# Average pooling over 536 MB: rows of 128 KB per partition, and every store in SyncE's queue

## The chip, the core and the metric

The kernel runs on one core of a Trainium2 chip. A core has a VectorE (DVE in the profile), a ScalarE (ACT), a GpSimd (POOL), a TensorE (PE, not used here) and a SyncE (SP), and sixteen DMA engines which move data between the DRAM and the core's own memory of 128 partitions. SyncE and ScalarE each have a DMA queue; a transfer put into either is spread over all sixteen DMA engines. The metric is the time of one execution in microseconds (us); the time given is the median of several executions. A profile of one further execution shows where the time goes.

## The reference

Each row of 8192 numbers is cut into groups of four, and each group is replaced by its mean. The input is 64 x 256 x 8192 float32 (536.87 MB), the output 64 x 256 x 2048 float32 (134.22 MB).

```python
def reference(x, kernel_size, stride):          # kernel_size = stride = 4
    batch, channels, length = x.shape
    out_len = (length - kernel_size) // stride + 1
    output = np.zeros((batch, channels, out_len), dtype=np.float32)
    for i in range(out_len):
        start = i * stride
        output[:, :, i] = np.mean(x[:, :, start : start + kernel_size], axis=2)
    return output
```

Since windows do not overlap and 8192 is a multiple of 4, the whole input can be treated as one flat line of numbers: every four neighbours give one output.

## The kernel before

The flat input is cut into 64 blocks of 8 MB. In a block each of the 128 partitions holds a run of `RUN` = 16384 numbers, 64 KB, and the runs of neighbouring partitions follow each other in DRAM, so a block is one contiguous stretch (line 35). Its output is 16 KB for each partition, 2 MB in all (line 36).

For a block there are four steps. `load` (line 41) takes a tile `xt` of 64 KB per partition out of a pool of two (line 38) and has SyncE issue the transfer (line 44). `sums` (line 47) has VectorE add neighbours twice: first 16384 numbers to 8192, written over the first half of `xt` itself (line 50), then 8192 to 4096, written into a result tile `r` (line 54). `scale` (line 58) has ScalarE multiply by a quarter in place (line 59). Then the result is stored.

Result tiles hold two blocks, 32 KB per partition, and come from a pool of two (line 39). The loop (line 68) goes over pairs of blocks. In the first four pairs (`SINGLES` = 8 blocks) each block is scaled and stored by itself, 2 MB, from ScalarE's queue (lines 74 and 75). In the others the pair is scaled by one call and stored by one transfer of 4 MB from ScalarE's queue (lines 77 and 78); in that transfer each partition has two rows of 16 KB, which lie 2 MB apart in DRAM (`both`, line 65).

The last three transfers of results are arranged otherwise. The pair of blocks 60 and 61 is scaled and stored late, from SyncE's queue, behind the last loads (lines 86 and 87). Block 62 is stored by itself (line 90). Block 63 is loaded in two pieces of 40 KB and 24 KB per partition (`LAST`, lines 84 and 85), and each piece is summed, scaled and stored as soon as it can be (lines 91 to 95).

The order on each engine is that of the program; waits between engines are put in by the framework from what each instruction reads and writes. So a load into a tile of `xt` waits until VectorE has finished both sums of the block that was in it two loads before, a scale waits for VectorE, a store for ScalarE, and VectorE's second sum waits until the result tile has been stored from its use two pairs before.

Of the kernel before, what the change touches and what calls it, by code (L numbers as in the profile page):

```python
# [1 line left out]

# [4 lines left out]


RUN = 16384

SINGLES = 8
LAST = (10240, 6144)


@with_exitstack
def kernel(
    ctx: ExitStack,
    tc: tile.TileContext,
    x: bass.AP,
    kernel_size: bass.AP,  # L20
    stride: bass.AP,
    out: bass.AP,
):
    nc = tc.nc
    K, S = int(kernel_size), int(stride)
    assert K == S == 4
    B, C, L = x.shape
    P = nc.NUM_PARTITIONS
    dt = x.dtype
    M = RUN // K  # L30
    blocks = B * C * L // (P * RUN)
    assert blocks * P * RUN == B * C * L and L % K == 0 and blocks % 2 == 0
    assert sum(LAST) == RUN

    xb = x.rearrange("b c l -> (b c l)").rearrange("(n p m) -> n p m", p=P, m=RUN)
    ob = out.rearrange("b c l -> (b c l)").rearrange("(n p m) -> n p m", p=P, m=M)

    pin = ctx.enter_context(tc.tile_pool(name="xin", bufs=2))
    pout = ctx.enter_context(tc.tile_pool(name="res", bufs=2))

    def load(i, a=0, b=RUN, xt=None):
        if xt is None:
            xt = pin.tile([P, RUN], dt, name="xt")
        nc.sync.dma_start(out=xt[:, a:b], in_=xb[i][:, a:b])
        return xt

    def sums(o, xt, a=0, b=RUN):
        v = xt[:, a:b].rearrange("p (m k) -> p m k", k=2)
        h = xt[:, a : (a + b) // 2]
        nc.vector.tensor_tensor(  # L50
            out=h, in0=v[:, :, 0], in1=v[:, :, 1], op=mybir.AluOpType.add
        )
        w = h.rearrange("p (m k) -> p m k", k=2)
        nc.vector.tensor_tensor(  # L54
            out=o, in0=w[:, :, 0], in1=w[:, :, 1], op=mybir.AluOpType.add
        )

    def scale(o):
        nc.scalar.mul(o, o, 1.0 / K)  # L59

    def edges(cuts):
        at = [sum(cuts[:j]) for j in range(len(cuts) + 1)]
        return list(zip(at[:-1], at[1:]))

    def both(i):
        return ob[i : i + 2].rearrange("n p m -> p n m")

    for i in range(0, blocks - 2, 2):
        r = pout.tile([P, 2, M], dt, name="r")
        for h in range(2):  # L70
            xt = load(i + h)
            sums(r[:, h, :], xt)
            if i < SINGLES:
                scale(r[:, h, :])
                nc.scalar.dma_start(out=ob[i + h], in_=r[:, h, :])
        if SINGLES <= i < blocks - 4:
            scale(r[:])
            nc.scalar.dma_start(out=both(i), in_=r[:])

    n = blocks - 1  # L80
    t = pout.tile([P, 2, M], dt, name="r")
    xt = load(n - 1)
    xl = None
    for a, b in edges(LAST):
        xl = load(n, a, b, xl)
    scale(r[:])
    nc.sync.dma_start(out=both(n - 3), in_=r[:])
    sums(t[:, 0, :], xt)
    scale(t[:, 0, :])
    nc.sync.dma_start(out=ob[n - 1], in_=t[:, 0, :])  # L90
    for a, b in edges(LAST):
        o = t[:, 1, a // K : b // K]
        sums(o, xl, a, b)
        scale(o)
        nc.sync.dma_start(out=ob[n][:, a // K : b // K], in_=o)


# [1 line left out]
_INS = ['x', 'kernel_size', 'stride']  # L99
_OUTS = [((64, 256, 2048), 'float32')]  # L100

_NUMBERS = {'kernel_size': 4, 'stride': 4}


# [26 lines left out]
```

## Time and profile before

| | |
|---|---|
| median of three runs | 1554.46 us (1554.44 to 1555.88) |
| the profiled execution | 1554.4 us |
| its span, from first to last instruction | 1552.6 us |
| bytes moved by DMA, and their rate over the span | 671.12 MB, 432 GB/s |
| first sum, `xt` from 128 x 16384 to 128 x 8192 | 63 times, 8692 ns each |
| second sum, into `r`, 128 x 4096 | 63 times, 4425 ns each |
| scale of two blocks, 128 x 8192 | 27 times, 7029 ns each |
| scale of one block, 128 x 4096 | 9 times, 3616 ns each |
| load of a block, from issue to landing | median 35.1 us |
| store of 4 MB from ScalarE's queue, from issue to landing | median 52.0 us |
| idle time of VectorE that a load ended | 696.1 us, 63 times |

The span is the time between the first and the last instruction on the core; the profiled execution's own time is 1.8 us longer. Busy times of engines overlap each other, so they are not added up. Of a DMA the profile shows the issue (a short instruction on the issuing engine), the packets (one for each contiguous piece that a DMA engine moves) and the landing. A queue's share is the time of its packets as a part of sixteen engines' span. In the profile, "q1" is SyncE's queue and "q10" ScalarE's.

### The profile page before, as it was taken

To read this page: it belongs to the slowest core of one execution; us is meant where nothing else is said; L and a number is where in the kernel's file an instruction comes from. 1 tells how busy PE (TensorE), PEld (TensorE's weight loads), DVE (VectorE), ACT (ScalarE), POOL (GpSimd) and SP (SyncE) were. 2 spreads that over 40 slices of the span, in tenths; PEclk is the share of its full clock that TensorE was granted. 3 is DMA by queue.
4 is the path that set the end of the run, shared out by engine and by line. 5 is a ranking of instruction groups with operands and counts; after the bars stand their busy time and mean duration, and the time that the engine had idled before them with its cause. 6 is when DMAs were issued, how large, how long until landed. Compare 5 with 4: busy or idle time off the path is not lost.

```text
span 1552.6 us, 471 instructions
## 1 busy us (share of the span) xinstructions
DVE 839.7 (54%) x130; ACT 227.4 (15%) x39; POOL 0.2 (0%) x4
## 2 busy tenths in 40 slices
DVE  3646556546465464654646546455464554645646
ACT  1111101110111101111011110111101111011111
POOL 0000000000000000000000000000000000000000
DMA  9999999999999999999999999999999999999999
GB/s 417 420 434 438 439 439 439 412 445 444 413 433 435 443 438 439 432 424 429 439 438 433 437 434 419 439 432 438 439 419 434 434 437 439 441 423 442 422 440 400
DMA packets 18292, 671.12 MB, mean 432 GB/s; under 512 B 1649, under 2 KB 1649, under 8 KB 1777
## 3 DMA queue, kind: packets, MB, share of 16 engines
q1 hardware_dynamic: 10064, 545.26, 81.1%
q10 hardware_dynamic: 8224, 125.83, 18.9%
q14 instruction: 4, 0.02, 0.0%
HBM read 536.87 MB, written 134.22 MB: 432 GB/s over the span
## 4 chain that ended last, share of the span: by engine, by line
DMA 71%; DVE 28%; issue 0%; ACT 0%; DVEq 0%
DMA xt<-in_x_dram 71%; DVE xt L50 18%; DVE r L54 9%; ACT r L59 0%; DVEq L54 0%
## 5 line engine op out<-in xcount | busy, mean ns | idle before, releaser
L50 DVE TENSOR_TENSOR xt<-xt 128x8192 f32<-128x8192 f32 (+1 forms) x65 | 556.5, 8561 | 696.1 <-DMA xt<-in_x_dram 696.1
L59 ACT ACTIVATE r<-r 128x8192 f32<-128x8192 f32 (+3 forms) x38 | 226.2, 5951 | 1313.0 <-DVE r L54 1313.0
L54 DVE TENSOR_TENSOR r<-xt 128x4096 f32<-128x4096 f32 (+1 forms) x65 | 283.4, 4360 | 3.9
L59 ACT ACT_TABLE_LOAD x1 | 1.3, 1283 | 0.7 <-PEq L112 0.7
L112 POOL MEMSET const-bfloat16-1.0<- 128x1 bf16 x1 | 0.1, 101 | 0.0
L112 POOL MEMSET const-uint8-127<- 128x1 uint8 x1 | 0.1, 101 | 0.0
L112 POOL MEMSET const-float32-0.0<- 128x1 f32 x1 | 0.1, 98 | 0.2 <-issue 0.2
L112 POOL MEMSET const-float32-1.0<- 128x1 f32 x1 | 0.1, 98 | 0.0
## 6 DMA issues: line engine op xcount, KB each, us to landing
out_dram<-r ACTq DMA_DIRECT2D x26, 4096.0 KB, 52.0
out_dram<-r ACTq DMA_DIRECT2D x8, 2048.0 KB, 31.7
xt<-in_x_dram SPq DMA_DIRECT2D x1, 5120.0 KB, 23.1
out_dram<-r SPq DMA_DIRECT2D x1, 4096.0 KB, 33.0
xt<-in_x_dram SPq DMA_DIRECT2D x1, 3072.0 KB, 30.0
out_dram<-r SPq DMA_DIRECT2D x1, 2048.0 KB, 16.9
out_dram<-r SPq DMA_DIRECT2D x1, 1280.0 KB, 12.9
xt<-in_x_dram SPq DMA_DIRECT2D x63, 35.1
```

The lines of the kernel that those rows point to most:

```text
L50: nc.vector.tensor_tensor(out=h, in0=v[:, :, 0], in1=v[:, :, 1], op=mybir.AluOpType.add)
L54: nc.vector.tensor_tensor(out=o, in0=w[:, :, 0], in1=w[:, :, 1], op=mybir.AluOpType.add)
L59: nc.scalar.mul(o, o, 1.0 / K)
L112: nc = _bacc.Bacc("TRN2", target_bir_lowering=False, num_devices=1)
```

## The change

The input is cut into 32 groups of 16 MB. In a group each partition holds a run of 128 KB of neighbouring numbers, and two loads fetch it: the first takes the first 64 KB of every partition's run, the second the second 64 KB. So the rows of one load now start 128 KB apart in DRAM and are no longer one contiguous stretch. The group's output is 32 KB per partition in one piece, and the 4 MB of a group are contiguous.

Each half is scaled by a call of its own, the groups at the start too. All stores are issued by SyncE; ScalarE issues no transfer any more. A group's store is held back and issued after the second load of the next group. At the end, the last group's second half is again loaded in pieces of 40 KB and 24 KB; behind these loads come the store of group 30, that of the first half of group 31, and those of the two pieces. The two sums, the tiles of `xt` and the sizes of the pools are as before.

```diff
--- before.py
+++ after.py
@@ -8,7 +8,6 @@
 
 RUN = 16384
 
-SINGLES = 8
 LAST = (10240, 6144)
 
 
@@ -28,20 +27,24 @@
     P = nc.NUM_PARTITIONS
     dt = x.dtype
     M = RUN // K
-    blocks = B * C * L // (P * RUN)
-    assert blocks * P * RUN == B * C * L and L % K == 0 and blocks % 2 == 0
+    groups = B * C * L // (2 * P * RUN)
+    assert groups * 2 * P * RUN == B * C * L and L % K == 0
     assert sum(LAST) == RUN
 
-    xb = x.rearrange("b c l -> (b c l)").rearrange("(n p m) -> n p m", p=P, m=RUN)
-    ob = out.rearrange("b c l -> (b c l)").rearrange("(n p m) -> n p m", p=P, m=M)
+    xb = x.rearrange("b c l -> (b c l)").rearrange(
+        "(n p h m) -> n h p m", p=P, h=2, m=RUN
+    )
+    ob = out.rearrange("b c l -> (b c l)").rearrange(
+        "(n p m) -> n p m", p=P, m=2 * M
+    )
 
     pin = ctx.enter_context(tc.tile_pool(name="xin", bufs=2))
     pout = ctx.enter_context(tc.tile_pool(name="res", bufs=2))
 
-    def load(i, a=0, b=RUN, xt=None):
+    def load(g, h, a=0, b=RUN, xt=None):
         if xt is None:
             xt = pin.tile([P, RUN], dt, name="xt")
-        nc.sync.dma_start(out=xt[:, a:b], in_=xb[i][:, a:b])
+        nc.sync.dma_start(out=xt[:, a:b], in_=xb[g, h][:, a:b])
         return xt
 
     def sums(o, xt, a=0, b=RUN):
@@ -62,37 +65,34 @@
         at = [sum(cuts[:j]) for j in range(len(cuts) + 1)]
         return list(zip(at[:-1], at[1:]))
 
-    def both(i):
-        return ob[i : i + 2].rearrange("n p m -> p n m")
+    def store(g, r, a=0, b=2 * M):
+        nc.sync.dma_start(out=ob[g][:, a:b], in_=r[:, a:b])
 
-    for i in range(0, blocks - 2, 2):
-        r = pout.tile([P, 2, M], dt, name="r")
-        for h in range(2):
-            xt = load(i + h)
-            sums(r[:, h, :], xt)
-            if i < SINGLES:
-                scale(r[:, h, :])
-                nc.scalar.dma_start(out=ob[i + h], in_=r[:, h, :])
-        if SINGLES <= i < blocks - 4:
-            scale(r[:])
-            nc.scalar.dma_start(out=both(i), in_=r[:])
+    held = None
+    for g in range(groups):
+        r = pout.tile([P, 2 * M], dt, name="r")
+        xt = load(g, 0)
+        sums(r[:, :M], xt)
+        scale(r[:, :M])
+        if g == groups - 1:
+            break
+        xt = load(g, 1)
+        if held is not None:
+            store(*held)
+        sums(r[:, M:], xt)
+        scale(r[:, M:])
+        held = g, r
 
-    n = blocks - 1
-    t = pout.tile([P, 2, M], dt, name="r")
-    xt = load(n - 1)
     xl = None
     for a, b in edges(LAST):
-        xl = load(n, a, b, xl)
-    scale(r[:])
-    nc.sync.dma_start(out=both(n - 3), in_=r[:])
-    sums(t[:, 0, :], xt)
-    scale(t[:, 0, :])
-    nc.sync.dma_start(out=ob[n - 1], in_=t[:, 0, :])
+        xl = load(g, 1, a, b, xl)
+    store(*held)
+    store(g, r, 0, M)
     for a, b in edges(LAST):
-        o = t[:, 1, a // K : b // K]
-        sums(o, xl, a, b)
-        scale(o)
-        nc.sync.dma_start(out=ob[n][:, a // K : b // K], in_=o)
+        a1, b1 = M + a // K, M + b // K
+        sums(r[:, a1:b1], xl, a, b)
+        scale(r[:, a1:b1])
+        store(g, r, a1, b1)
 
 
 # ---- launch: one core; inputs and outputs as the reference has them ----
```

## The prediction

> **What bounds the kernel now.** I read the page first, then a table of busy times by stretch, then the timeline of one steady group, then SyncE's waits, and last the trace's own packet records (one for each descriptor that a DMA engine moved: start, duration, bytes, queue). The page:
>
> ```profile
> span 1552.6 us, 471 instructions
> DVE 839.7 (54%) x130; ACT 227.4 (15%) x39; POOL 0.2 (0%) x4
> ...
> DMA packets 18292, 671.12 MB, mean 432 GB/s; under 512 B 1649, under 2 KB 1649, under 8 KB 1777
> ...
> q1 hardware_dynamic: 10064, 545.26, 81.1%
> q10 hardware_dynamic: 8224, 125.83, 18.9%
> ...
> DMA xt<-in_x_dram 71%; DVE xt L50 18%; DVE r L54 9%; ACT r L59 0%; DVEq L54 0%
> ```
>
> SP's queue (q1) and ACT's queue (q10) together take 81.1 + 18.9 = 100% of the sixteen DMA engines. VectorE is busy 54% of the time, ScalarE 15%. The chain names VectorE for 27% only because a load waits for its buffer; while it waits, the other buffer's load is under way. The stretches show whether any stage escapes this (columns: from:to, us, busy time and count on each engine, clock, DMA share, GB/s):
>
> ```profile
> core 0: us, DVE busy (x) ACT busy (x) POOL busy (x), PEclk, DMA share, GB/s
> 3.00:22.00 19.00, 0.00 (x0) 0.00 (x0) 0.00 (x0) 1.00 0.98 424
> 250.00:1450.00 1200.00, 651.75 (x100) 174.69 (x25) 0.00 (x0) 1.00 1.00 433
> 1531.00:1550.00 19.00, 8.58 (x4) 3.82 (x2) 0.00 (x0) 1.00 1.00 427
> ```
>
> The first stretch has loads alone, the middle one loads and stores mixed, the last one stores alone (the last load's packets end at 1531.8). All three have a DMA share of 0.98 to 1.00. Short stretches blur at their edges, where a packet is counted whole, so 424 and 427 are not slower than 433. A steady group:
>
> ```profile
> 1018.97 48.08 SPq L44 DMA_DIRECT2D xt<-in_x_dram  x3
> 1018.98 7.03 ACT L59 ACTIVATE r<-r 128x8192 f32<-128x8192 f32 x1 [41.94 <-DVE r L54]
> 1026.04 0.38 ACTq L78 DMA_DIRECT2D out_dram<-r  x1
> 1029.36 8.69 DVE L50 TENSOR_TENSOR xt<-xt 128x8192 f32<-128x8192 f32 x1 [10.42 <-DMA xt<-in_x_dram]
> 1038.14 4.42 DVE L54 TENSOR_TENSOR r<-xt 128x4096 f32<-128x4096 f32 x1
> 1053.54 8.69 DVE L50 TENSOR_TENSOR xt<-xt 128x8192 f32<-128x8192 f32 x1 [10.97 <-DMA xt<-in_x_dram]
> ```
>
> Two blocks arrive every 1077.91 - 1029.36 = 48.5 us (the next pair's start on VectorE is 1077.91); VectorE needs 13.2 us for each and idles 10 to 11 us before each, waiting for a load. So the kernel is a pipe filled from end to end, and only two things can move its time: the cost of the packets, or a hole between them.
>
> **Packets, which the change does alter.** In the records a 64 KB load packet takes 2418 ns (median of 8064), a 16 KB store packet 611 (8064 of them). On one engine the next packet starts about 4 ns before the last one's end, so they cost 2414.3 and 607.3 ns. The line through these two is 1807.0 ns for 48 KB, so 602.3 ns for 16 KB and 5.0 ns fixed for each packet. The records' 24 KB, 10 KB and 6 KB packets (912, 385, 234 ns) lie on the same line.
>
> Removed: the stores of 16 KB rows. Added: 31 stores of 128 rows of 32 KB. The records have no 32 KB packet; by the line one costs 2 x 602.3 + 5.0 = 1209.6 ns, in place of 2 x 607.3 = 1214.6. The last group keeps 16 KB and smaller rows, as before. Each engine has 31 x 128 / 16 = 248 such packets: 248 x 5.0 = **1.2 us less**. Bounds: nothing, if a row is cut into two packets again; and 248 x 8.7 = 2.2 us, if the whole 8.7 ns by which the 611 exceeds its 602.3 counts. I take 1.2, since the start-to-start spacing is what fills the span. Stores fall from 38 to 34; each has one 9 ns semaphore packet per engine, so this is under 0.04 us.
>
> **Addresses of the loads.** Rows stay 64 KB, but start 128 KB apart in DRAM, not 64 KB. No transfer of before has that pitch. Nearest row: the loads of before, 2418 ns in 98% of the records, and after 210 us only 3 of some 7000 take over 2425. Lower bound: no change. Upper bound from rows: the 2% of slow ones after the first round average 2465 ns; all 512 per engine at that are +24 us. I take nothing, since 64 KB within a row stays contiguous and that is what one packet reads.
>
> **One queue, and the place of the store.** ACT now issues no DMA. SP's order becomes load (g,0), load (g,1), store g-1, load (g+1,0). What must hold is that each is issued before its turn. Call T the landing of load (g,0). With 8 packets a load is 8 x 2.414 = 19.3 us, a store 8 x 1.210 = 9.7, so the cycle is 48.3 us. Load (g,1) needs the buffer of (g-1,1), which landed at T - 29.0 and is summed 13.2 us later: issued at T - 15.8, turn at T. Store g-1 needs 3.62 us of ScalarE more (the half tile's row) and some 0.4 us: issued at T - 11.7, turn at T + 19.3. Load (g+1,0) is issued when (g,0) is summed, T + 13.2, turn at T + 29.0. The least lead is **15.8 us**, against 0.9 us from the first load's issue (0.73) to its first packet (about 1.65). So SP's new wait for ScalarE costs nothing: behind it stands load (g+1,0), which could not go before T + 13.2 anyway. If that cover were gone (a sum of 29 us in place of 13.2), each further microsecond would be a hole in every group, 31 us in all. VectorE's write into the result tile of g+1 needs store g-1 out; that store stands ahead of load (g+1,0) in one queue, so it is out 19 us earlier.
>
> ScalarE: 65 halves and pieces in place of 38 calls, 62 x 3.62 + 3.62 + 2.34 + 1.48 = 232 us in place of 226, under its 1313 us of waiting. VectorE's instructions are unchanged.
>
> Boundaries between DMAs in one queue: load to load 2 to 37 ns, load to store in the tail 2.1, store to store 1.8. Store to load within one queue does not occur in before; across the two queues it costs -3.7. I take 2 ns, with 31 of them, nothing. Lower bound nothing; upper bound the 0.9 us of a fresh start, 31 x 0.9 = +28 us.
>
> Start and end: the first two loads go as before. After the last load 4 + 2 + 1.25 + 0.75 MB of stores remain, as before, some 19 us of packets; the last piece is issued at 1541.2 and its packets begin at 1548.5, so 7 us of cover stay.
>
> **Sum.** Span 1552.6 - 1.2 = 1551.4. The profiled execution took 1554.4, so 1.8 lie around the span: 1553.2. It stands 0.06 under the median of the runs, 1554.46; so **1553.3**.
>
> **Rivals.**
> *A, slower: the 128 KB pitch makes load packets longer.* For it: engines run nearly in step (the starts of sixteen packets fall within 0.6 us), so their rows' addresses stay a fixed power of two apart, and the very first round, all engines at once, took 2415 to 3462 ns. Against it: the loads of before run in step at another power of two and show nothing. It decides from about 8 ns a packet (4.3 us over 512). With the commonest slow value of the records, 2439, it is 512 x 21 = 10.8 us, so 1564; with 2465, 1577.
> The Trainium skill (DMA: Bandwidth & Descriptors, Latency and other measured facts) lists copies whose per-partition row pitch is a large power of two: 207 GB/s at 512 KiB against 214 padded, 164 at 2 MiB. Its smallest pitch is four times this one; at its 3% the loads' 1238 us would grow by an estimated 41 us, to 1594. No run here shows that pitch.
> *B, slower: a hole at each change of direction in the single queue.* Before, packets of two queues alternate, so an engine always has the other queue's packet at hand. In one queue the load behind a store might start only when the store's writes are acknowledged. For it: that boundary was never run. Against it: store to store in the tail, with a semaphore between, shows 1.8 ns. It decides from (3.1 + 1.2)/31 = 0.14 us a group; at 0.9 us it is 28 us, 1581.
> *C, faster by over 3.1 us.* At the bare 37.65 ns per KB (1807.0/48) each engine's 40960 KB take 1542.0 us; the active time is some 1549.7. Of those 7.7 us, 5 are fixed packet cost, of which 1.2 go. It would need the slow first round and the spread at the end to vanish also. Time about 1551.
> *D: the 32 KB rows are cut into 16 KB packets,* so that nothing changes: 1554.4. Against it: 64 KB rows go as one packet.
>
> **Chances.** Forecast 0.53, D 0.04, A 0.24, B 0.14, C 0.05. A measurement of this kernel can tell about 0.2%, 3.1 us, from no change; forecast and D lie inside: 0.57 same, 0.38 slower, 0.05 faster. The likeliest case's own range is 1552 to 1555. To leave out no more than 2 in 10 the range takes A up to about three quarters of its cases and the lower part of B: 1552 to 1572.
>
> **What would show it.** Right: 32 KB packets at about 1213 ns and 64 KB ones at 2418, ten thousand odd packets all in q1, a DMA share of 1.00 throughout, VectorE's starts a load's 19.3 us and then 29 us apart by turns, SP's waits ended by VectorE and by loads. A shows as 64 KB packets over 2425 ns without holes; B as store-to-load gaps with packets at 2418. A slice of DMA share below 9 tenths in the middle would refute the leads.

## The result: slower by 0.24%

The changed kernel takes 1558.25 us (median of 14 runs, 1557.32 to 1559.43), the kernel before 1554.45 (14 runs). The ratio is 1.0024, 95% interval 1.0015 to 1.0032: a small loss, but clear of the noise. The profiled execution took 1557.59 us with a span of 1555.8, which is 3.2 more than before. The forecast was 1553.3 us, 1.2 less than before.

The page of the changed kernel:

```profile
span 1555.8 us, 463 instructions
DVE 839.6 (54%) x130; ACT 232.9 (15%) x66; POOL 0.2 (0%) x4
...
DMA packets 14259, 671.12 MB, mean 431 GB/s; under 512 B 1584, under 2 KB 1584, under 8 KB 1712
...
q1 hardware_dynamic: 14256, 671.09, 99.8%
...
DMA xt<-in_x_dram 71%; DVE xt L53 18%; DVE r L57 9%; ACT r L62 0%; DVEq L57 0%
```

All packets but a few are in SyncE's queue, and there are some 4000 fewer. Of the sixteen engines' span 99.8% is still packets, and the chain has the same shares as before. So no hole opened, and the page shows nothing of where 3.2 us went. In the table of stretches (columns as before) the middle is full as it was:

```profile
250.00:1450.00 1200.00, 654.00 (x100) 177.19 (x49) 0.00 (x0) 1.00 1.00 434
1534.00:1553.00 19.00, 8.55 (x4) 3.82 (x2) 0.00 (x0) 1.00 0.92 393
```

Only the last stretch differs: 0.92, where the kernel before had 1.00 at about the same distance from its end. The packet records below show that some engines end later than others.

What SyncE waited for shows that the leads held. Two lines of before, then three of the changed kernel:

```profile
SPq L44 <- DVE r L54: 817.2, 62, 13.2
SPq L44 <- DMA xt<-in_x_dram: 660.1, 62, 21.1
...
SPq L47 <- DVE r L57: 817.2, 62, 13.2
SPq L47 <- DMA xt<-in_x_dram: 548.6, 62, 21.0
SPq L69 <- ACT r L62: 141.0, 34, 28.6
```

Its wait for VectorE before a load is the same 817.2 us, 62 times, as before. The timeline tells more. Here are starts of VectorE's first sum in the changed kernel, each of which is a load's landing: the second to the fifth, and then three in the steady part:

```profile
41.99 8.69 DVE L53 TENSOR_TENSOR xt<-xt 128x8192 f32<-128x8192 f32 x1 [6.20 <-DMA xt<-in_x_dram]
61.35 8.69 DVE L53 TENSOR_TENSOR xt<-xt 128x8192 f32<-128x8192 f32 x1 [6.20 <-DMA xt<-in_x_dram]
81.50 8.69 DVE L53 TENSOR_TENSOR xt<-xt 128x8192 f32<-128x8192 f32 x1 [7.00 <-DMA xt<-in_x_dram]
110.64 8.69 DVE L53 TENSOR_TENSOR xt<-xt 128x8192 f32<-128x8192 f32 x1 [16.00 <-DMA xt<-in_x_dram]
...
1003.52 8.69 DVE L53 TENSOR_TENSOR xt<-xt 128x8192 f32<-128x8192 f32 x1 [6.13 <-DMA xt<-in_x_dram]
1032.54 8.69 DVE L53 TENSOR_TENSOR xt<-xt 128x8192 f32<-128x8192 f32 x1 [15.86 <-DMA xt<-in_x_dram]
1051.88 8.69 DVE L53 TENSOR_TENSOR xt<-xt 128x8192 f32<-128x8192 f32 x1 [6.13 <-DMA xt<-in_x_dram]
```

A load alone takes 61.35 - 41.99 = 19.36 us, and later 1051.88 - 1032.54 = 19.34. But the load that landed at 81.50 took 20.15, 0.8 too long. It is the load just ahead of the first store. In the steady part a store and a load take 1032.54 - 1003.52 = 29.02 us, and two landings of like place are 1051.88 - 1003.52 = 48.36 apart, as in the kernel before (48.35 in the mean). Now the first and the last whole load, of before and then of the changed kernel:

```profile
22.73 8.69 DVE L50 TENSOR_TENSOR xt<-xt 128x8192 f32<-128x8192 f32 x1 [22.73 <-DMA xt<-in_x_dram]
1513.12 8.69 DVE L50 TENSOR_TENSOR xt<-xt 128x8192 f32<-128x8192 f32 x1 [11.21 <-DMA xt<-in_x_dram]
...
22.64 8.69 DVE L53 TENSOR_TENSOR xt<-xt 128x8192 f32<-128x8192 f32 x1 [22.64 <-DMA xt<-in_x_dram]
1516.09 8.69 DVE L53 TENSOR_TENSOR xt<-xt 128x8192 f32<-128x8192 f32 x1 [15.86 <-DMA xt<-in_x_dram]
```

The first lands as early as before, the last 3 us later. Since the steady part keeps the old pace, the loss lies in the earlier part of the run.

The packet records say which packets. Slow are called load packets of 64 KB that took over 60 ns more than 2418, the first round left out. Each engine also ends its share of a DMA with a 4-byte packet; for one DMA the time between the first and the last of these sixteen is called the spread of the engines. The last row is how far the slowest engine's 4-byte packet lies behind the mean of the sixteen.

```
                        before    changed
slow load packets           30        102   (88 of the 102 in the load just ahead of a store)
their excess, us per engine 0.28      2.19
spread at the last load, us 1.02      3.84
slowest engine over mean    0.74      2.44
```

In the changed kernel the spread climbs with the turns: 0.45 at the first store, 1.73 after three more, 2.54, 2.78, 3.10, 3.6, 3.8, and there it stays from 710 us on. Engines that have fallen behind do not catch up, and the kernel ends with the slowest: 2.19 - 0.28 = 1.9 more in the mean and 2.44 - 0.74 = 1.7 more for the slowest over the mean make 3.6, against 3.2 in the span.

The records do not name the engine. But each packet starts some 4 ns before the end of the one ahead of it, so they can be put in order engine by engine. In that order 85 of the 88 are the very last load packet ahead of their engine's first store packet.

### The profile page after: what moved, and what is told of

Read it like the earlier page. It is cut to its first block, busy times and chain, and to the rows that moved or that the text cites. A ratio compares the mean times of both kernels' runs of the same rounds, so it can differ in the third digit from the quotient of the medians.

```text
span 1555.8 us, 463 instructions
## 1 busy us (share of the span) xinstructions
DVE 839.6 (54%) x130; ACT 232.9 (15%) x66; POOL 0.2 (0%) x4
## 3 DMA queue, kind: packets, MB, share of 16 engines
q1 hardware_dynamic: 14256, 671.09, 99.8%
## 4 chain that ended last, share of the span: by engine, by line
DMA 71%; DVE 28%; issue 0%; ACT 0%; DVEq 0%
DMA xt<-in_x_dram 71%; DVE xt L53 18%; DVE r L57 9%; ACT r L62 0%; DVEq L57 0%
## 5 line engine op out<-in xcount | busy, mean ns | idle before, releaser
L62 ACT ACTIVATE r<-r 128x4096 f32<-128x4096 f32 (+1 forms) x65 | 231.6, 3564 | 1310.5 <-DVE r L57 1310.5
```

## The experiments

The ratios are to the kernel before, run on the same chip.

**One queue or the pitch?** Theory Q: the turn from loads to stores in the single queue. Theory P: the 128 KB pitch. Two kernels have one of them each, a third doubles the turns, a fourth has no turns.

*The pitch without the single queue* (`e1_act_queue`; `store` is told its queue).

```diff
...
-        if held is not None:
-            store(*held)
         sums(r[:, M:], xt)
         scale(r[:, M:])
         held = g, r
+        if g < groups - 2:
+            store(g, r, q=nc.scalar)
...
```

> The changed kernel's rows (loads at a pitch of 128 KB, stores of 32 KB rows), but the stores of groups 0 to 29 go into ScalarE's queue as soon as they are scaled. Theory Q (the loss of about 3.8 us comes where the single queue turns all engines from loads to stores: the last load packets before a store take 60 to 920 ns longer, some engines lose more than others, and the slowest ends last): no such turns, spread of the engines at the end about 1 us, about 1553.3. Theory P (the pitch of 128 KB slows load packets, whatever the queue): spread above 3 us and 1557.3 to 1559.4, as the changed kernel.

Measured: 1580.94 us (1568.39 to 1583.97), ratio 1.0152 (1.0122 to 1.0182). Neither theory has this: 27.6 us above the forecast of 1553.3, not 4 or 5. The six runs lie far apart, and the profiled one (1583.90) is among the slowest. Its timeline:

```profile
1028.89 8.69 DVE L53 TENSOR_TENSOR xt<-xt 128x8192 f32<-128x8192 f32 x1 [16.84 <-DMA xt<-in_x_dram]
1045.72 0.34 ACTq L69 DMA_DIRECT2D out_dram<-r  x1
1048.17 8.69 DVE L53 TENSOR_TENSOR xt<-xt 128x8192 f32<-128x8192 f32 x1 [6.13 <-DMA xt<-in_x_dram]
1078.33 8.69 DVE L53 TENSOR_TENSOR xt<-xt 128x8192 f32<-128x8192 f32 x1 [16.95 <-DMA xt<-in_x_dram]
```

Landings of like place are 1078.33 - 1028.89 = 49.4 us apart where 48.35 is the rate of the pipe, so a group loses about 1 us. And the place of the loss can be seen in the table of issues:

```profile
out_dram<-r ACTq DMA_DIRECT2D x30, 4096.0 KB, 33.9
```

A store takes 33.9 us of the 49.4, so each group has some 15 us of loads alone, and then the stores set in again. In the records 783 load packets are slow, 26.8 us per engine, most of the 29.5 by which this span is longer than before; the engines' spread has the rest. For one store, issued at 996.32, the slow ones start from 996.1 to 1003.0, take up to 3711 ns in place of 2418, and there are no more until the next store is due. Put in order by engine, 432 of the 480 load packets that stand last ahead of a store's first packet are slow, by 621 ns in the mean of all; of the two ahead of each, 143 are, and 167 of the 476 that come right behind that first store packet. Two packets further on, between one 32 KB store packet and the next, it is 4 of 473. So it isn't the size of the store packets that slows the loads beside them.

*The single queue without the pitch* (`e2_old_rows`): the blocks and rows of before in the order of the changed kernel. `store` here is SyncE's, with the two rows of `both(i)`.

```diff
...
-                nc.scalar.dma_start(out=ob[i + h], in_=r[:, h, :])
-        if SINGLES <= i < blocks - 4:
-            scale(r[:])
-            nc.scalar.dma_start(out=both(i), in_=r[:])
+        xt = load(i + 1)
+        if held is not None:
+            store(*held)
+        sums(r[:, 1, :], xt)
+        scale(r[:, 1, :])
+        held = i, r
...
```

> The blocks and rows of before (loads of contiguous 8 MB, stores of two rows of 16 KB), but in the order of the changed kernel: all in SyncE's queue, a pair's store behind the second load of the next. Theory Q: 1557 to 1560 (1.2 us above the changed kernel for the smaller store packets, less or more by chance), spread of the engines 3 us or more at the end. Theory P: 1554.4, spread about 1 us.

Measured: 1559.07 us (1558.36 to 1560.03), ratio 1.0030 (1.0019 to 1.0041); spread 3.93, 123 slow load packets, 112 of them in the load ahead of a store. The loss is there without the pitch. Theory P falls for the changed kernel.

*Twice as many turns* (`e3_half_stores`).

```diff
         xt = load(g, 0)
+        if held is not None:
+            store(*held, 0, M)
...
-            store(*held)
+            store(*held, M, 2 * M)
...
```

> The changed kernel with each half's 2 MB stored by itself, behind the first and the second load of the next group: 62 turns from loads to stores in place of 31, stores of 16 KB rows. Theory Q, if each turn costs the same: about 2 x 5 - 1.2 us over 1553.3, some 1560 to 1563; if the loss stops once the engines are spread: as the changed kernel plus 1.2, 1558 to 1560. Theory P: 1558 to 1560 too, but with slow load packets anywhere in a load and not gathered at the turns.

Measured: 1558.94 us (1557.61 to 1559.84), ratio 1.0028 (1.0017 to 1.0039). The spread climbs by turns, reaches 3.34 at the twelfth and stays. So the loss is not so much per turn: it fills up and stops.

*No turns* (`e4_no_stores`): the stores of groups 0 to 29 left out, so most of the output is not written.

> The changed kernel without the stores of groups 0 to 29, which are left out. Loads are 63 x 19.31 + 12.1 + 7.3 = 1236 us, the last stores 19.3, start and end some 4: about 1259 to 1260 if every load packet takes its 2.414 us. Theory P: slow load packets remain, spread 3 us or more, 1262 to 1265. Theory Q: no turn, so spread of the engines under 1 us and 1259 to 1260.5.

Measured: 1264.75 us (1264.53 to 1265.06), above theory Q's times and within those of theory P. But the spread is 1.18 (theory Q had under 1, theory P 3 or more) and only 3 load packets are slow, so it isn't P. My sum was too small: it had 4 us for start and end, while first round, spread, end and the time around the span come to over 6, and it had 2414 ns for a load packet. Here, without any stores, the packets of a load start 2418 ns apart; in the kernel before, where they alternate with stores, 2414.2.

**What is it about the stores that slows loads?** Theory O: the onset, when engines begin to store after a stretch of loads alone. The kernel before has no onsets after its first stores: its stores take 52.0 us at a period of 48.4, so the next is issued while the last is still under way.

```profile
out_dram<-r ACTq DMA_DIRECT2D x26, 4096.0 KB, 52.0
```

Sixteen 16 KB store packets on each engine alternate with sixteen load packets. With 32 KB rows there are only eight, and the alternation stops halfway. Theory P2: in ScalarE's queue it is the pitch after all.

*The pitch with stores that fill the period* (`x1_act_16k_rows`): each half stored by itself from ScalarE's queue.

```diff
+        if g < groups - 2:
+            store(g, r, 0, M, nc.scalar)
         xt = load(g, 1)
...
+        if g < groups - 2:
+            store(g, r, M, 2 * M, nc.scalar)
...
```

> The changed kernel's loads (pitch of 128 KB), but each half of a result is stored by itself, in rows of 16 KB, from ScalarE's queue as soon as it is scaled: 8 store packets on each engine for 8 load packets, so loads and stores alternate without a pause. Theory O (what costs is the onset: load packets that are in flight when the engines begin to store after a stretch of loads alone take up to 1.3 us longer): no onsets after the first, 1554 to 1555.5. Theory P2 (in ScalarE's queue the pitch of 128 KB is what costs, so the first experiment's 27 us come from it): 1575 to 1585.

Measured: 1555.44 us (1555.18 to 1555.82), ratio 1.0006 (0.9996 to 1.0015). The 27 us are gone, with the pitch still there.

*The old loads with 32 KB rows* (`x2_act_32k_old_loads`).

```diff
-SINGLES = 8
+SINGLES = 0
...
-        return ob[i : i + 2].rearrange("n p m -> p n m")
+        return og[i // 2]
...
```

> The loads of before (contiguous 8 MB), every pair scaled by one call and stored from ScalarE's queue as 128 rows of 32 KB; so the outputs of a pair stand in another order in DRAM than the reference's. 8 store packets for 16 load packets: the stores are done halfway through the period and begin anew in each. Theory O: an onset in each pair, 1570 to 1585. Theory P2: no pitch of 128 KB, so 1553 to 1554.

Measured: 1568.02 us (1564.19 to 1569.86), ratio 1.0084 (1.0070 to 1.0098), with 436 slow load packets, 11.6 us per engine. The onset costs without the pitch, though half of what it cost in the first experiment, and a little less than expected.

*The switch half way* (`x3_switch_half_way`): the kernel of before up to block 31, then the single queue.

```diff
+FIRST = 32
...
-    for i in range(0, blocks - 2, 2):
...
+    for i in range(0, FIRST, 2):
...
+    for i in range(FIRST, blocks, 2):
...
```

> The kernel of before up to block 31 (half of the run, loads and stores in two queues), from block 32 on all in SyncE's queue as in e2_old_rows. Theory O: the onsets begin at 780 us, and the spread of the engines grows from 1 us or less to 3 us or more within the ten turns after it; 1557 to 1559.5. Theory E (the loss belongs to the first few hundred microseconds of a run, since that is where it was seen): spread stays at 1 us, 1554.4 to 1555.

Measured: 1557.98 us (1557.39 to 1558.61), ratio 1.0023 (1.0013 to 1.0032). The spread of a load is 0.7 to 1.5 up to the switch and 0.92 at it, then climbs with the turns: 3.38 at the ninth, 3.79 at the end. So the loss belongs to the first turns, not to the first microseconds of a run.

*Engines out of step from the start* (`x4_staggered`).

```diff
+        if g == 0:
+            for s in (0, 4):
+                nc.sync.dma_start(out=r[s : s + 4, :], in_=xb[0, 0][s : s + 4, : 2 * M])
...
```

> The changed kernel, with two extra transfers at the start that use four engines alone (2 x 32 KB for each, 2.4 us; the data go to a result tile that is overwritten later). Theory O with its limit (engines that reach the turn at different times no longer slow each other): the slips fill up to the same spread of 3 to 4 us, so about 1557 to 1559.5, as the changed kernel. If the slips come on top whatever the stagger: spread 5.5 to 6.5 us and 1560 to 1562.

Measured: 1562.60 us (1562.42 to 1563.13), ratio 1.0053 (1.0041 to 1.0066): by its time this is the rival's, or a little above. But the transfers did more than was meant: the first packets of 64 KB took up to 7011 ns, and the first landing came 30.80 - 22.64 = 8.2 us later than in the changed kernel:

```profile
30.80 8.69 DVE L53 TENSOR_TENSOR xt<-xt 128x8192 f32<-128x8192 f32 x1 [30.80 <-DMA xt<-in_x_dram]
```

By the end of the span only 1561.0 - 1555.8 = 5.2 of these are left, so 3 us less were lost on the way. The spread began at 3.06 and rose by only 1.2 to 4.28, and 30 load packets were slow, 0.36 us per engine, in place of 102 and 2.19. That speaks for the limit; since the start was disturbed as well, I take it as support and not as proof.

**Why 1581 and 1568?** The first experiment and the one with the old loads differ in the pitch, and in the moment of the store, since one scale of 7.03 us for both halves delays it. The next kernel (`y1_act_32k_one_scale`) is the first experiment's with one scale.

```diff
-        scale(r[:, :M])
...
-        scale(r[:, M:])
+        scale(r[:])
...
```

> As e1_act_queue (loads at a pitch of 128 KB, 32 KB rows stored from ScalarE's queue), but with one scale for both halves, so that the store is issued 3.4 us later in the period, as in x2_act_32k_old_loads. If the difference between those two (1580.9 and 1568.0) comes from the time of the onset within a load: 1564 to 1570. If it comes from the pitch: 1575 to 1585.

Measured: 1569.37 us (1567.47 to 1571.51), ratio 1.0095 (1.0081 to 1.0108). It isn't the pitch, which this kernel has. The median is 12 us below the first experiment's, as it would be if the moment counted. But two of that kernel's six runs, 1568.39 and 1570.70, lie in this one's range, with their store as early as in the others; so the moment is not shown to be the cause. Here the store is issued just as the load lands (first line the issue, second the landing):

```profile
1039.66 0.34 ACTq L69 DMA_DIRECT2D out_dram<-r  x1
1039.95 8.69 DVE L53 TENSOR_TENSOR xt<-xt 128x8192 f32<-128x8192 f32 x1 [7.38 <-DMA xt<-in_x_dram]
```

In the first experiment it was issued 1048.17 - 1045.72 = 2.45 us before the landing.

*All blocks stored singly, old loads* (`y2_all_singles`; `SINGLES = 60`).

> The kernel of before with every block up to 59 scaled and stored by itself from ScalarE's queue (SINGLES = 60), as x1_act_16k_rows has it, but with contiguous loads. If the 1.0 us of x1_act_16k_rows over before comes from its pitch: 1554.3 to 1554.6. If it comes from the stores of 2 MB each: 1555.2 to 1555.8.

Measured: 1555.61 us (1555.40 to 1555.92), ratio 1.0006 (0.9997 to 1.0015), as with the pitch of 128 KB (1555.44). Here stores of 2 MB take 31.7 us at a period of 24.2, so they never pause either:

```profile
out_dram<-r ACTq DMA_DIRECT2D x60, 2048.0 KB, 31.7
```

The 1.0 us over before is inside both intervals; as far as it is real, it belongs to the stores and not to the pitch. In both kernels the one late engine (spread 1.9 at the end, 1.0 before; one 24 KB load packet of 1511 to 1513 ns in place of 912) appears where the last 4 MB go to the other queue. The pitch of 128 KB costs nothing that can be measured, here or between 1569.37 us with it and 1568.02 without, whose ranges overlap. No version here that writes all its results beats the kernel before.

## Why the prediction was wrong

**What bounds the kernel** was right. The DMA engines are full in both kernels, and no engine's work showed.

**The step that failed** is that of the boundaries between DMAs in one queue: "I take 2 ns, with 31 of them, nothing". The gaps between packets are indeed nothing: behind a store the next load packet starts 2 ns after the store packet's end. But I had looked for the price in the gaps alone, and it is in the duration of the load packets just ahead of a store. Rival B had the change of direction, but the wrong boundary (a load behind a store) and the wrong shape (a hole at each turn, 31 times the same). The runs show slower packets on the way from loads to stores, mostly at the first ten or so turns, and an end set by the slowest of sixteen engines: 1.9 us in the mean and 1.7 of spread.

The records of before held a sign of it. At the first store of that kernel, issued at 39.56, ten load packets that started within 0.7 us took 2474 to 2658 ns. I had noted the slow 2% as a matter of addresses. (Their commonest value is 2429, not the 2439 that rival A is priced with; that gives 512 x 11 = 5.6 us and 1559 in place of 1564. And the first load packet starts at 1.74, so a fresh start is 1.0 us, not 0.9.) I also read ScalarE's store of 52 us at a period of 48.4 as a queue that is merely busy; it is what keeps the loads and stores alternating without an onset.

**The packets.** The 32 KB packets took 1213 ns, as the line gave. But the saving of 0.04 us a group did not arrive: over the last ten groups a group took 48.35 us, over the last fifteen pairs of before the same. In order by engine, load packets of the steady part start 2415.7 ns apart in the mean, against 2414.2 before. Over the 14 such steps of a group that is some 21 ns, about half of the saving. Where the rest went is not worked out. I had taken 2414.3 for all.

**The leads** were right: VectorE's starts are 19.34 and 29.02 us apart by turns (19.3 and 29.0 forecast), and SyncE's waits before loads did not grow. **The pitch** was right at nothing, and rival A falls: two pairs of kernels with and without it lie within 1.4 us, and one of them within 0.2. The Trainium skill (DMA: Bandwidth & Descriptors, Latency and other measured facts) has 207 GB/s at a pitch of 512 KiB against 214 padded, some 3% less. No run here shows that pitch, and at 128 KB nothing near 3% was seen. **Rivals C and D** did not occur: no packet was cut.

**The range** of 1552 to 1572 held the time, since it reached to A and the lower part of B; its likeliest case, 1552 to 1555, did not. That the time fell inside is luck: neither rival is what happened.

## What to carry to other kernels

Where the DMA engines set the end, count the packets of each queue on one engine over a period, and see whether loads and stores alternate all the time or in bouts; a store whose landing time exceeds its period never pauses. In two queues the kernels whose stores pause were 13 to 26 us slower than the kernel before, those whose stores don't some 1 us; in one queue, where loads and stores come in bouts, it was about 4. Fewer and larger store packets looked cheaper by 5 ns each, and in two queues they broke that match. A trace's page shares say nothing of it: look at the durations of single packets around the first store, and at how far the sixteen engines have drifted apart at the end.

## What the runs showed of the hardware

- The 64 KB load packets around an engine's first store packet after a stretch of loads alone, above all the last one ahead of it, take up to 1.9 us longer (4289 ns at most in the first experiment, against 2418). In the kernel before, where loads and stores alternate, 98% of the load packets take some 2418.
- In a single queue this stops when the engines are 3.3 to 3.9 us apart (four kernels; 4.3 in the one with the disturbed start). In two queues it doesn't: the spread comes to swing between 3.4 and 7.6 us (three kernels), and the loss comes in every group.
- A load pitch of 128 KB in DRAM cost nothing measurable: 1555.44 us with it, 1555.61 without.

What in the chip makes a load wait there (its own engine's store beside it, or the memory on either side) was not tried and stays open; so does what picks the engines that fall behind, and why runs of the first experiment lie 15 us apart. In two queues, stores that pause always had 32 KB rows here and stores that don't 16 KB rows; only the order of the slow packets separates the two, not a kernel of its own.
